# Raw attention rows staged in the weights' rooms, branch weights loaded three ahead, and the place of the last token block's norm

## The chip, the cores and the metric

The kernel runs on one core of a Trainium2 chip. The metric is the device time of one execution in microseconds (us). Three runs of the kernel before took 1567.14, 1567.76 and 1568.34 us, so the median is 1567.76. TensorE is called PE here, VectorE DVE, ScalarE ACT, GpSimd POOL, and SyncE, which issues most transfers, SP.

## The reference

One layer of an encoder on a sequence of 1024 tokens with 1024 channels, in float32. What the change touches is in the merge of the two branches and in the norm ahead of the MLP:

```
h = rmsnorm(x, g_mix)                       # z = h @ w_in -> pooling channels, q, k, v
y_pool = pool_mixer(u_pool, ...)            # 512 channels
y_attn = diff_attention(q, k, v, ...)       # 8 heads x 128 channels, each head's output RMS-normed, * g_sub * 0.8
gates  = sigmoid(h @ w_gate + b_gate)
merged = gates[:, :D] * (y_pool @ w_branch_pool) + gates[:, D:] * (y_attn @ w_branch_attn)
x  = x + merged @ w_out
h2 = rmsnorm(x, g_ffn)                      # x * rsqrt(mean(x*x) + 1e-6) * g_ffn
x  = x + square(relu(h2 @ w_up)) @ w_down
```

## The kernel before

Every float32 operand of a product is split into a high part (a cast on ACT) and a low part (the difference, on DVE or POOL; `split`, L115), and every product is three matmuls: high by high, high by low, low by high (`mm3`, L120, whose three lines L123 to L125 carry nearly all rows of PE).

**Stages.** First the attention runs head by head (8 heads, 8 token blocks of 128 each), with its stages overlapped over the blocks. While it ends, PE also computes the pooling channels and the 16 column tiles of the gates (`gate_cols`), whose results go to DRAM. Then come, in this order: `branch_pool` for the eight output tiles d of the pooling branch (rows `bp`); the attention branch for the eight tiles d (rows `ba`), each with a contraction over the eight heads' tiles `yT[0]` to `yT[7]`, in two halves of 512 tokens; the output projection (rows `op`); the norm ahead of the MLP; the MLP's up projection in 16 column pairs and its down projection. Both MLP projections use Strassen's scheme with seven products (numbered 1 to 7) on blocks of the normed input: 11, 21 and the combinations T1, T2, T3, 22 and T4.

**From the attention to `yT`.** A head's unnormed output goes to DRAM as rows of `y_dram`, and its norm's factors, one per token, as a row of `r_dram` (`stage_norm`, L600; the factors' store is L614). In the loop at L798 each tile is read back: `load_split` (L189) loads raw y (512 KB) into a `raw` tile, loads the head's row of factors broadcast over all partitions (`rb`, L198), scales raw y by them and by `gs` on DVE (L199), and splits it into two tiles `yT`.

**Rooms.** A tile pool has a fixed number of rooms for each tag, and an instruction that writes a new tile waits until a room of the tag is free. `raw` has 2 rooms and serves all raw weights of these stages (`rbp`, `rba`, `ro`), the raw pooling outputs (`rypT`) and raw y (`ryT`). Split weights lie in 8 rooms "W" and 4 rooms "fw" of 4 KB a partition; `wt` (L129) gives the first 64 tiles (the attention's) W rooms, and then by turns 8 tiles W and 4 tiles fw. The gates' weights also use the four fw rooms, with raw rooms of their own (`fr`, two, L142). The factors `rb` use a U room of the attention's (11 of these, which `yT` 0 to 4 use too), the single room `fu`, or two half rooms `fr` and `fo` by `tmp`; `yT` 5 to 7 go to rooms of a pool that is opened when the attention has ended.

**Weights of the attention branch.** `load_cols` loads one tile of `w_branch_attn`; tiles 0, 1 and 2 are loaded in the loop at L798 (L801 to L803), and the loop at L811 loads tile d + 2 for each d, so tile 2 is loaded and split twice.

**The norm ahead of the MLP.** `norm_token` (L903) takes a token block: two squares with sums on ACT, the sum and mean on DVE (L912), EPS added on DVE and the power -1/2 on POOL (`rsq`, L246), a scaling on ACT (L914), the product with the gain row `gfb` on DVE (L917), and eight transposes on PE (L920). `second_half` calls it for blocks 4 to 7 and makes T1 and T2 of a block from the transposed halves and from what `first_half` put into DRAM; `combine` (L989) then makes T1's split, T3, 22 and T4 of all four blocks, on DVE with casts on ACT. The loop at L1111 traces the beginnings of the first four pairs and a call of `combine` behind each.

**The order of the work.** The order on each engine's queue is set when the program is built. A planner runs the program by times of its own and gives each engine, among the instructions that are ready in its time, the one that stands earliest in the program; `tc.cur_priority` moves a piece of program to an earlier place. On the chip each queue then goes in that fixed order, SP's included, and an instruction that has to wait holds all behind it. The last pair of the up projection has its place noted as `last_pair` (L1127), and the first three operand sets of the down projection (`early`, L1255) are given this place.

## Time and profile before

| What | Value |
|---|---|
| median of three runs | 1567.76 us (1567.14 to 1568.34) |
| span of the profiled execution | 1565.6 us |
| the profiled execution's time beside the span | not given by the page; the span is the figure that it has |
| mean granted TensorE clock | 0.996 |
| PE busy | 1536.9 us, 98% of the span |
| DVE, ACT, POOL busy | 1016.4, 817.6 and 357.3 us |
| DMA | 206.94 MB, mean 132 GB/s |

The span runs from the first to the last instruction of one execution, and times in rows are us from its start. A row of a timeline gives start, duration, engine, line, operation, result and operands with buffer numbers left out, shape and count, and in brackets how long the engine had idled and what released it. A row of the list of waits gives total us, times and longest. `SPq` and `ACTq` are issues of transfers; their duration is that of the issue, not of the transfer. PE's matmuls are pipelined: their starts, not their durations, give the pace.

### The profile page before, as it was taken

What the parts mean: (1) busy time and instruction counts of PE and PEld (TensorE: products, weight loads), DVE (VectorE), ACT (ScalarE), POOL (GpSimd) and SP (SyncE); (2) the same over time, 40 slices, a digit from 0 to 9 for tenths busy, and PEclk for the clock granted to TensorE, in tenths of its full rate; (3) what the DMA queues carried; (4) which work ended last, traced back from release to release, by engine and by line L of the source; (5) the groups of instructions that cost most, each with busy time, mean ns of one, the idle gap of its engine ahead of it and who ended that gap; (6) DMA issues with size and microseconds to landing.
All of it is one profiled execution on the core that took longest, in us unless ns stands there. A gap on an engine that the chain in (4) does not pass through costs nothing.

```text
span 1565.6 us, 22082 instructions
## 1 busy us (share of the span) xinstructions
PE 1536.9 (98%) x7649; PEld 1322.5 (84%) x7649; DVE 1016.4 (65%) x2277; ACT 817.6 (52%) x1810; POOL 357.3 (23%) x449
## 2 busy tenths in 40 slices
PE   7999999999999999999799999999999999999999
PEld 6899999999999989888688887888888788888887
DVE  6777677777878797743542358776666568546572
ACT  6656556656565655544542546565555634333331
POOL 5433333343434252222454400000000000000000
PEclk9999999999999999999899999999999999999999
DMA  7111212121112121256645633555342699537650
GB/s 227 50 52 48 64 46 62 34 64 52 60 44 67 35 89 40 69 158 207 205 143 177 193 115 117 182 166 185 132 141 108 247 316 381 197 121 252 218 195 27
DMA packets 168010, 206.94 MB, mean 132 GB/s; under 512 B 10118, under 2 KB 104027, under 8 KB 167899
## 3 DMA queue, kind: packets, MB, share of 16 engines
q1 hardware_dynamic: 150490, 178.23, 35.3%
q10 hardware_dynamic: 17408, 27.30, 4.7%
q8 instruction: 60, 0.98, 0.3%
q14 instruction: 52, 0.42, 0.1%
HBM read 150.94 MB, written 54.56 MB: 131 GB/s over the span
## 4 chain that ended last, share of the span: by engine, by line
PE 49%; DVE 1%; ACT 1%; DMA 1%; issue 1%; POOLq 0%; DVEq 0%
PE Da L124 4%; PE Da L123 4%; PE Da L125 4%; PE Db L124 3%; PE Db L123 3%; PE Db L125 3%; PE X L123 3%; PE X L124 3%; PE X L125 3%; PE ba L124 2%; PE op L123 2%; PE op L125 2%; PE op L124 2%; PE ba L125 2%; PE ba L123 2%; PE Z L123 2%
## 5 line engine op out<-in xcount | busy, mean ns | idle before, releaser
L123 PE MATMUL z<-wqkv,hT 128*128 128x384 f32 x512 | 174.5, 341 | 0.5 <-DVE qn L441 0.3
L125 PE MATMUL z<-wqkv,hT 128*128 128x384 f32 x512 | 174.3, 341 | 0.5 <-DVE hT L118 0.4
L124 PE MATMUL z<-wqkv,hT 128*128 128x384 f32 x512 | 173.6, 339 | 0.0
L510 ACT ACTIVATE s<-s,nm 128x256 f32<-128x256 f32 (+7 forms) x128 | 99.6, 778 | 48.9 <-DVE nm L502 44.0
L249 POOL TENSOR_TENSOR ms<-ms,mhalf 128x4 f32<-128x4 f32 x64 | 67.4, 1053 | 157.8 <-DVE ms L248 139.3
L125 PE MATMUL g<-hT,fwgate 128*128 128x512 f32 x256 | 101.0, 394 | 0.0
L124 PE MATMUL g<-hT,fwgate 128*128 128x512 f32 x256 | 100.9, 394 | 0.0
L123 PE MATMUL g<-hT,fwgate 128*128 128x512 f32 x256 | 100.9, 395 | 0.0
L123 PEld LDWEIGHTS z<-wqkv,hT 128*128 128x128 f32 x512 | 96.8, 189 | 4.2 <-DVE qn L441 1.0
L125 PEld LDWEIGHTS z<-wqkv,hT 128*128 128x128 f32 x512 | 96.6, 189 | 3.1 <-DVE hT L118 1.3
L124 PEld LDWEIGHTS z<-wqkv,hT 128*128 128x128 f32 x512 | 96.7, 189 | 2.9
L502 DVE CUSTOM_DVE_ANT_0 s<-sc,dist 128x512 f32<-128x512 f32 (+3 forms) x128 | 74.7, 586 | 22.1 <-PE sc L500 20.7
L118 DVE TENSOR_TENSOR AS<-s,AS 128x512 fp32r<-128x512 f32 x64 | 43.9, 689 | 36.7 <-ACT AS L117 36.5
L118 POOL TENSOR_TENSOR wqkv<-rqkv,wqkv 128x384 fp32r<-128x384 f32 x60 | 63.1, 1071 | 19.6 <-ACT wqkv L117 19.3
L499 PE MATMUL sc<-K,Q 128*128 128x512 f32 (+2 forms) x192 | 67.2, 355 | 0.1
L500 PE MATMUL sc<-K,Q 128*128 128x512 f32 (+2 forms) x192 | 66.6, 354 | 0.0
L473 ACT CAST Q<-tk 64x128 fp32r<-64x128 f32 x128 | 33.2, 259 | 58.6 <-DVE Q L472 56.8
L447 POOL TENSOR_TENSOR qn<-qn,ggh 128x128 f32<-128x128 f32 x64 | 32.3, 505 | 137.7 <-DVE qn L441 119.5
L470 ACT CAST Q<-tk 64x128 fp32r<-64x128 f32 x128 | 33.0, 258 | 50.1 <-DVE K L469 48.7
L123 PE MATMUL ba<-yT,wba 128*128 128x512 f32 x128 | 51.7, 404 | 7.6 <-ACT yT L117 7.6
L118 POOL TENSOR_TENSOR fwgate<-frgate,fwgate 128x512 fp32r<-128x512 f32 x32 | 45.0, 1408 | 53.7 <-ACT fwgate L117 53.5
L125 PEld LDWEIGHTS g<-hT,fwgate 128*128 128x128 f32 x256 | 48.1, 188 | 8.6
(429 smaller groups left out, 4659.6 us busy)
## 6 DMA issues: line engine op xcount, KB each, us to landing
wd<-in_w_down_dram SPq DMA_DIRECT2D x56, 512.0 KB, 5.6
wu<-in_w_up_dram SPq DMA_DIRECT2D x32, 512.0 KB, 5.0
udS<-us SPq DMA_DIRECT2D x64, 256.0 KB, 2.3
ur<-udS SPq DMA_DIRECT2D x32, 512.0 KB, 3.4
rqkv<-in_w_in_dram SPq DMA_DIRECT2D x64, 192.0 KB, 2.8
ud<-u ACTq DMA_DIRECT2D x48, 256.0 KB, 3.9
ur<-ud SPq DMA_DIRECT2D x24, 512.0 KB, 3.9
frgate<-in_w_gate_dram SPq DMA_DIRECT2D x32, 256.0 KB, 2.7
```

Source lines behind the costliest of these rows:

```text
L118: (lo_eng or nc.vector).tensor_tensor(lo, src, f(hi), op=ALU.subtract)
L123: nc.tensor.matmul(ps, lhs_hi, rhs_hi, start=first, stop=False, **kw)
L124: nc.tensor.matmul(ps, lhs_hi, rhs_lo, start=False, stop=False, **kw)
L125: nc.tensor.matmul(ps, lhs_lo, rhs_hi, start=False, stop=last, **kw)
L249: nc.gpsimd.tensor_tensor(dst, dst, mhalf[:, :n], op=ALU.pow)
L447: nc.gpsimd.tensor_tensor(qn[:, 2:4, :], qn[:, 2:4, :], ggh.unsqueeze(1).broadcast_to([P, 2, HD]), op=ALU.mult)
L470: nc.scalar.copy(q_hi, q)
L473: nc.scalar.copy(Q[other, m, 1, :], q)
L499: nc.tensor.matmul(dst, Q[:, i, 0, :], rhs, start=True, stop=False)
L500: nc.tensor.matmul(dst, Q[:, i, 1, :], rhs, start=False, stop=True)
L502: nc.vector.tensor_tensor_reduce(out=s[i][:, c : c + w], in0=sc[:, 0:w], in1=dist[:, o0 + c : o0 + c + w], scale=2.0 ** -(h + 1), scalar=B ...
L510: nc.scalar.activation(s[i][:, 0:n], s[i][:, 0:n], AF.Exp, bias=last, scale=-1.0, accum_out=Z[:, i, t : t + 1])
```

## The change

- Raw y gets W rooms instead of `raw` (`y_scaled`). Tiles 0 to 3 are loaded and scaled at once behind the first pooling weights in program order, and each tile d + 4 behind the split of tile d. The factors of tiles 0 to 3 and 5 use `fu`, those of 4 a U room, those of 6 and 7 the half rooms.
- The turns of W and fw rooms behind the attention are written out (`ROOMS`, one letter for two tiles): two pooling pairs in W, two in fw, then three attention tiles in W, two in fw and three in W.
- The loop over the attention branch loads tile d + 3 instead of d + 2, so that tile 2 is loaded once.
- `norm_token` computes (sum + D * EPS) to the power -1/2 with one DVE step; the missing factor, the root of D, is multiplied into `gfb` once.
- The instructions of `combine` for T3, 22 and T4 are put behind the last norm's scaling on ACT and its gain product on DVE in these queues (`tc.issue_after`: an order on the same engine, no wait for an end).
- `up_pair` has one more yield behind the copies of products 6 and 5 (U2 and z5). For the last pair the loop steps to this point before `last_pair` is noted.

```diff
+ROOMS = "WWFFWWWFFWWW"
+N_AHEAD_Y = 4
@@ def wt
-        if wcount[0] > N_QKVW and (wcount[0] - N_QKVW - 1) % (N_W + N_FW) >= N_W:
+        if wcount[0] > N_QKVW and ROOMS[(wcount[0] - N_QKVW - 1) // 2] == "F":
             return fw_tile(shape, name)
@@ def load_split
-    def load_split(src, r0, name, tile_fn, scale=None):
-
-        rw = raw([P, S], f"r{name}")
-        nc.sync.dma_start(rw, src[r0 : r0 + P, :])
-        if scale is not None:
-            rbs, row = scale
-            n = S // len(rbs)
-            for i, rb in enumerate(rbs):
-                js = slice(i * n, (i + 1) * n)
-                nc.sync.dma_start(rb, row[js].partition_broadcast(P))
-                nc.vector.scalar_tensor_tensor(rw[:, js], rw[:, js], gs, rb, op0=ALU.mult, op1=ALU.mult)
+    def split_halves(rw, name, tile_fn):
+
         ts = []
         for th in range(2):
             t = tile_fn([P, 2, 512], F32R, f"{name}_{th}", th)
             split(t[:, 0, :], t[:, 1, :], rw[:, th * 512 : (th + 1) * 512])
             ts.append(t)
         return ts
+
+    def load_split(src, r0, name, tile_fn):
+
+        rw = raw([P, S], f"r{name}")
+        nc.sync.dma_start(rw, src[r0 : r0 + P, :])
+        return split_halves(rw, name, tile_fn)
+
+    def y_scaled(d, rbs):
+
+        rw = wpool.tile([P, S], F32, tag="W", name=f"ry{d}", bufs=N_W)
+        nc.sync.dma_start(rw, y_dram[d * P : (d + 1) * P, :])
+        n = S // len(rbs)
+        for i, rb in enumerate(rbs):
+            js = slice(i * n, (i + 1) * n)
+            nc.sync.dma_start(rb, r_dram[d][js].partition_broadcast(P))
+            nc.vector.scalar_tensor_tensor(rw[:, js], rw[:, js], gs, rb, op0=ALU.mult, op1=ALU.mult)
+        return rw
@@
+    def row_factors(d):
+        if d < N_AHEAD_Y or d == 5:
+            return [fu_tile(f"rb{d}")]
+        if d == 4:
+            return [ut([P, S], F32, f"rb{d}")]
+        return [tmp(f"rb{d}_{i}") for i in range(2)]
+
     ws_bp = {0: load_cols2(w_branch_pool, 0, "bp0")}
+    ys = {d: y_scaled(d, row_factors(d)) for d in range(N_AHEAD_Y)}
     ypT = [load_split(p_dram, g * P, f"ypT{g}", ypt_tile) for g in range(4)]
@@
         branch_pool(d, ws_bp[d - d % 2][d % 2], bank)
-        if d % 4 < 2:
-            rb = [fu_tile(f"rb{d}") if d % 2 else ut([P, S], F32, f"rb{d}")]
-        else:
-            rb = [tmp(f"rb{d}_{i}") for i in range(2)]
-        yT.append(load_split(y_dram, d * P, f"yT{d}", yt_tile(d), (rb, r_dram[d])))
+        yT.append(split_halves(ys.pop(d), f"yT{d}", yt_tile(d)))
+        if d + N_AHEAD_Y < NK:
+            ys[d + N_AHEAD_Y] = y_scaled(d + N_AHEAD_Y, row_factors(d + N_AHEAD_Y))
     mT = {}
     for d in range(NK):
-        if d + 2 < NK:
-            ws_ba[d + 2] = load_cols(w_branch_attn, (d + 2) * P, f"ba{d + 2}")
+        if d + 3 < NK:
+            ws_ba[d + 3] = load_cols(w_branch_attn, (d + 3) * P, f"ba{d + 3}")
@@
     nc.sync.dma_start(gfb, g_ffn[0].partition_broadcast(P))
+    nc.vector.tensor_scalar(gfb, gfb, float(D) ** 0.5, None, op0=ALU.mult)
@@ def norm_token
-        nc.vector.tensor_scalar(rs, ss[:, 0:1], ss[:, 1:2], 1.0 / D, op0=ALU.add, op1=ALU.mult)
-        rsq(rs, rs, 1, 1.0)
-        nc.scalar.activation(yn, yn, AF.Copy, scale=rs)
+        nc.vector.tensor_scalar(rs, ss[:, 0:1], ss[:, 1:2], D * EPS, op0=ALU.add, op1=ALU.add)
+        nc.gpsimd.tensor_tensor(rs, rs, mhalf[:, 0:1], op=ALU.pow)
+        last["act"] = nc.scalar.activation(yn, yn, AF.Copy, scale=rs).ins
         for j, b in enumerate(ps):
             js = slice(j * 512, (j + 1) * 512)
-            nc.vector.tensor_tensor(yn[:, js], yn[:, js], gfb[:, js], op=ALU.mult)
+            last["dve"] = nc.vector.tensor_tensor(yn[:, js], yn[:, js], gfb[:, js], op=ALU.mult).ins
@@ def up_pair
         nc.scalar.copy(z5, Z)
+        yield
         sub(dve, S3, A["11"], A["21"])
@@
-        combine(q)
+        with ExitStack() as behind:
+            if q != "T1":
+                for e in last.values():
+                    behind.enter_context(tc.issue_after(e))
+            combine(q)
@@
         if p == NP - 1:
+            next(pairs[p])
             last_pair = tc.cur_priority
```

More of the change, by code (lines that the diff above doesn't have):

```diff
@@ L901, in b_split @@
         split(hi[:, :, c0 : c0 + P], lo[:, :, c0 : c0 + P], src, eng)
+    last = {}
     def norm_token(t, bank_fn):
```

## The prediction

> **What bounds the kernel now.** I read the page's busy shares first, then the list of what TensorE (PE) waited for.
>
> ```profile
> span 1565.6 us, 22082 instructions
> PE 1536.9 (98%) x7649; PEld 1322.5 (84%) x7649; DVE 1016.4 (65%) x2277; ACT 817.6 (52%) x1810; POOL 357.3 (23%) x449
> ```
>
> ```profile
> PE ba L123 <- ACT yT L117: 7.6, 1, 7.6
> PE Z L123 <- ACT BT1h L117: 2.8, 1, 2.8
> PE X L123 <- ACT U L1071: 1.6, 1, 1.6
> ```
>
> PE is busy 98% of the span, so a gain can only be idle or slowed PE time. These waits (total us, times, longest), with one of 1.4 us at the same `ba` product that its timeline shows below, are all above 1 us besides the start of the kernel, which the change doesn't touch. They stand at three places, and the diff has an edit for each: the branch product `ba` waits for `yT`, product 5 (`Z`) waits for the last token's `BT1`, the last pair's product 7 (`X`) waits for the copy U2. I take the places one by one, each from PE's timeline (start, duration, engine and line, idle before and its releaser).
>
> **Place 1, the y tiles.** The first `ba` product runs, stops before its eighth k, and starts again slowly:
>
> ```profile
> 745.11 0.40 PE L123 MATMUL ba<-yT,wba 128*128 128x512 f32 x1
> ...
> 749.30 0.40 PE L123 MATMUL ba<-yT,wba 128*128 128x512 f32 x1
> ...
> 757.94 0.80 PE L123 MATMUL ba<-yT,wba 128*128 128x512 f32 x1 [7.58 <-ACT yT L117]
> 760.10 0.80 PE L124 MATMUL ba<-yT,wba 128*128 128x512 f32 x1 [1.37 <-DVE yT L118]
> ...
> 765.27 0.39 PE L124 MATMUL ba<-yT,wba 128*128 128x512 f32 x1
> ```
>
> The row at 749.30 is the 18th start after 745.11: 4.19 / 18 = 0.233 us each. The row at 765.27 is the 34th, which at that pace would start at 745.11 + 34 x 0.233 = 753.03. So this place costs 765.27 - 753.03 = **12.2 us**: 7.58 + 1.37 of waiting and some 3.3 of slow matmuls. The windows show the slow clock, and none after the 2.8 us wait of place 2 (columns: length, then busy PE, PEld, DVE, ACT, POOL with counts, granted clock, DMA share, GB/s):
>
> ```profile
> 750.00:760.00 10.00, 1.15 (x3) 0.29 (x1) 5.58 (x8) 6.49 (x11) 2.94 (x2) 0.74 0.64 201
> 950.00:960.00 10.00, 8.44 (x39) 6.11 (x37) 8.29 (x15) 3.84 (x6) 3.87 (x1) 1.00 0.10 28
> 960.00:970.00 10.00, 8.79 (x38) 7.12 (x39) 7.22 (x12) 8.52 (x17) 0.00 (x0) 1.00 0.38 110
> ```
>
> The late tile is the eighth. Its raw y shares two `raw` rooms with the branch weights, so its load is issued after PE already needs it:
>
> ```profile
> 668.55 0.34 SPq L198 DMA_DIRECT2D rb<-r_dram  x1
> 669.42 0.37 SPq L671 DMA_DIRECT2D frgate<-in_w_gate_dram  x1
> ...
> 750.25 0.32 SPq L192 DMA_DIRECT2D ryT<-y_dram  x1
> ```
>
> The change takes raw y out of `raw`. When can the eighth be ready now? Its data is complete when head 7's factors are stored, and a load, one scale and a split follow:
>
> ```profile
> 708.87 0.29 ACTq L614 DMA_DIRECT2D r_dram<-rT  x1
> ```
>
> ```profile
> ryT<-y_dram SPq DMA_DIRECT2D x8, 512.0 KB, 4.9
> rb<-r_dram SPq DMA_DIRECT2D x4, 512.0 KB, 3.9
> ```
>
> ```profile
> 698.77 1.28 DVE L199 SCALAR_TENSOR_TENSOR ryT<-ryT,gs,rb 128x1024 f32<-128x1024 f32 x1 [3.52 <-DMA ryT<-y_dram]
> ```
>
> The store's landing isn't shown; 4.9 us, the time of the far larger y load, is my upper bound. 708.87 + 0.29 + 4.9 + 3.9 + 1.28 and as much again for the split is 720.5, some 30 us before PE asks for it near 750. Rooms: weights of head 7 leave eight W rooms, which hold bp0 (2), y0 to y3 and bp2 (2); y4 to y7 follow into the rooms of y0 to y3 as these are split. Even four loads strictly one behind the other, 4 x 4.9 = 19.6 from that store, with 2.6 of scale and split behind them, end some 19 us ahead of the need. That W rooms could be taken from a head's weights too early I exclude: the U room for y0's factors, a row written in head 0, was only granted at 668.55, so rooms are handed out in program order. I take the whole 12.2; the bounds are 0 (nothing arrives sooner) and 12.2.
>
> What is late next there: the weights `ba`, which now have `raw` to themselves and start earlier. Dropping the second load of tile 2 takes away one 512 KB transfer, two casts and two GpSimd (POOL) subtractions that no PE wait names: 0, and at most 0 to 1 if POOL became late. The same four scales and eight splits now run while PE does the gates, before 700. PE had no wait there; if every scale delayed an attention step that PE has in its queue, it would be 4 x 1.28 = 5.1. I take 0, since the gate products fill in, and keep 5.1 for the range.
>
> **Place 2, the last token's norm.**
>
> ```profile
> 939.43 0.69 DVE L845 TENSOR_TENSOR y<-op,y 128x512 f32<-128x512 f32 x1 [3.21 <-PE op L125]
> 942.24 0.59 ACT L910 ACTIVATE nsq<-y 128x512 f32<-128x512 f32 x1
> 943.64 1.29 DVE L118 TENSOR_TENSOR BT3l<-y,BT3h 128x512 fp32r<-128x512 f32 x2
> 948.46 0.21 DVE L912 TENSOR_SCALAR nrs<-nss 128x1 f32<-128x1 f32 x1
> 950.99 0.14 DVE L248 TENSOR_SCALAR nrs<-nrs 128x1 f32<-128x1 f32 x1
> 955.18 1.16 ACT L914 ACTIVATE y<-y,nrs 128x1024 f32<-128x1024 f32 x1 [4.06 <-POOL nrs L249]
> 956.37 1.29 DVE L917 TENSOR_TENSOR y<-y,gfb 128x512 f32<-128x512 f32 x2 [1.63 <-ACT y L914]
> 957.21 1.23 PE L920 MATMUL hb<-identf,y 128*128 128x128 f32 x8
> ```
>
> ```profile
> L249 POOL TENSOR_TENSOR nrs<-nrs,mhalf x8: 545/550/3872, 877.2 to 951.3; 128x1 f32<-128x1 f32 x8
> ```
>
> The second fence is the power on POOL, min/median/max in ns with its last start. The token is complete at 940.12, and its second square starts 2.1 us later, its sum 5.6 us after that, the second small VectorE (DVE) step 2.5 us later still: queues full of combinations and operand splits. The edit drops that second step (its 0.14 and the 2.5 of queue in front of it) and puts the combinations T3, 22 and T4 behind the norm on ACT and DVE. Operand splits and T1 stay ahead. In DVE's queue between 940.0 and 948.4 stand 14 operations; four are combinations (the two at 943.64 and two of `B22`), ten stay, and at 0.60 apart are 6.0 us: the sum comes by 946.2 at the latest, the end of a 3.87 us power by 950.1, that of scaling (1.16), the two products with the gain (1.29) and the eight transposes (1.23) by 953.8; a subtraction, a cast and a split of some 0.69 each make `BT1` by 955.9. PE runs out of work at 957.21 + 1.23 = 958.44. So the 2.8 us go. Against it stands the deferred work: 20 combination operations of 0.60 are 12 us of DVE that now start near 952 instead of 943. DVE idled 20 - 8.29 - 7.22 = 4.5 us between 950 and 970, which is about what can be caught up, and half of the 9 us shift remains to be met by order. I charge 0.8 us for product 4 (T4) coming late and take **2.0**, bounds 2.8 and, if PE then waits for the other half, 2.8 - 4.5 = -1.7.
>
> The last power took 3.87 us, seven times its peers' 0.55, and ended at 955.15; DVE's queue was full until 956.37 - 1.63 = 954.74, as the row of the gain product shows. The Trainium skill, SBUF — State Buffer, section "SBUF: two separate sides", says that GpSimd and VectorE share one pair of ports, held exclusively for a whole instruction when VectorE reads two SBUF inputs. By that rule every DVE queue that is full when the power starts holds it again, here too, and the 3.87 in my sum stays; without it 0.55 would do and the chain would end 3.3 us earlier. Both lie ahead of 958.4, so the sum is the same, but by the rule another 2.6 us of full queue on top would bring the wait back.
>
> Multiplying the gain row by 32 once costs at most the 1.28 of a two-input operation of that size; it lies in the output projection, in which PE waits for nothing: 0, at most 1.3.
>
> **Place 3, the last pair.**
>
> ```profile
> 1244.08 1.04 ACT L117 CAST u_3h<-ur 128x1024 fp32r<-128x1024 f32 x1
> 1245.02 1.04 ACT L117 CAST w_0h<-wd 128x1024 fp32r<-128x1024 f32 x1
> ...
> 1247.86 0.57 ACT L1071 COPY U<-X 128x512 f32<-128x512 f32 x1
> ```
>
> ```profile
> 1248.48 0.50 PE L123 MATMUL X<-BT3h,AS 128*128 128x512 f32 x1 [1.59 <-ACT U L1071]
> ```
>
> Three weight casts of the down projection (w_0 to w_2) stand ahead of the copy that frees `X`. With the new yield those operands rank behind U2 and z5. If the copy goes in front of w_0 it ends at 1245.6, before PE's need at 1248.48 - 1.59 = 1246.9: the whole 1.6. `u_3`, which ranks lower still, went first because it was ready, so one or two casts can stay ahead; with two, 0.8 is left. I take **1.4**, bounds 0 and 1.6. The down projection's first operands move back by two copies, some 1.1 us, which PE's remaining products cover.
>
> **Sum.** 12.2 + 2.0 + 1.4 = 15.6. The span 1565.6 becomes 1550.0. The page gives no time beside the span; the three runs shown have a median of 1567.76, 2.2 more than the profiled span, which I leave unchanged: **1552.2 us**.
>
> **Rivals.** *The y wait only shrinks* (0.11): the new order of SyncE's queue (SP) leaves y7 5 us late instead of 9. For it: SP waits in order, and factors 0 to 3 and 5 pass through one `fu` room. Against it: 30 us of margin. Then 4 us of wait and up to 3.3 of slow clock stay of 12.2: 5 gained, 1567.8 - 5 - 3.4 = 1559.4. The Trainium skill, TensorE: Matmul & The Clock Gate, Part 1, puts the idle time that halves the clock at about 3.4 us, between the 2.8 and 7.6 seen here; by it a rest below that would cost no clock, 3.3 less.
>
> *The combinations become the bound* (0.10): place 2 gives -1.7, and the pair behind it, whose operands DVE makes as well, is late by 2 more, my estimate; 1567.8 - 12.2 - 1.4 + 3.7 = 1557.9. For it: the deferred 12 us; against it the 4.5 idle.
>
> *The change doesn't do what it says* (0.06): the planner, which orders by its own clock, still issues y4 to y7 late; only places 2 and 3 gain, 1564.4, or nothing, 1567.8.
>
> *A hold on SP* (0.08), the side of slower. With factors 0 to 3 in one room, each factor load waits on SP for the scale before it: 3.9 + 1.28 and, as my estimate, 1.8 of gaps, 7 us a step. If three steps stand ahead of the gate load that was issued at 669.42, it comes 21 us late.
>
> ```profile
> 676.83 1.29 POOL L118 TENSOR_TENSOR fwgate<-frgate,fwgate 128x512 fp32r<-128x512 f32 x1 [1.41 <-ACT fwgate L117]
> 682.17 0.69 ACT L745 ACTIVATE go<-g,cols 128x512 f32<-128x512 f32 x1 [1.66 <-PE g L125]
> ```
>
> Those weights were done at 678.1; PE ended the product before at 682.1 and needs their second half 12 matmuls of 0.233 later, at 684.9: 6.8 us of slack. PE then waits 14.2 and pays 3.3 of clock: 1552.2 + 17.5 = 1569.7, with a fourth step 1576.7. It decides from a hold of 19.1 us (6.8 + 15.6 - 3.3). Against it: factor 0 can be loaded long before the W rooms come free, so that the steps can be over before 669.
>
> **How the numbers follow.** My forecast has 0.65, and its own range is 1550.8 to 1555.5 (all three waits whole: 1567.8 - 16.6 = 1551.2, with the runs' half spread; nothing from place 3 and 0 from place 2: 1555.5). To leave out no more than 0.2 with the unknown delays among the gates (5.1 more is 1557.3) the range reaches over the first two rivals to 1561: 1550.5 to 1561. A measurement of this kernel can tell about 0.2%, 3.1 us. Faster by more: 0.65 + 0.11 + 0.10 and half of the third, 0.89; within it the other half and a hold of three steps, 0.06; slower a hold of four or the like elsewhere, 0.05.
>
> **What would show it.** Right: no `ba` wait on `yT` and a clock of 1.00 throughout; raw y loads before 725; PE's wait for `BT1` and for U2 gone from the list. Wrong: a PE wait on `g` or `bp` near 680 to 735 (the SP hold), on `BT4` or `BT3` behind 965 (the combinations), or y7 loaded behind 740. A new wait of over 3 us anywhere would make the forecast wrong, above all in the gates, whose order is planned anew.

## The result, and the profile after

The changed kernel takes a median of 1556.93 us (1556.57 to 1557.44, five runs) against 1567.76 before (1566.17 to 1568.87, five runs): a ratio of 0.9933, 95% interval 0.9921 to 0.9945. It is 10.8 us faster. That lies above the forecast of 1552.2 and its own range (to 1555.5), and within the full range (to 1561.0). The profiled execution took 1556.93 us and has a span of 1555.1, 10.5 less than before.

In the kernel after, lines are shifted: `mm3` is L125 to L127, `split` L119 and L120, the norm L929 to L939, the copy U2 L1090. PE is now busy 99% of the span. This is the list of what it waited for (total us, times, longest):

```profile
PE X L125 <- ACT U L1090: 1.5, 1, 1.5
PE Z L125 <- ACT BT1h L119: 1.4, 1, 1.4
...
PE Y L125 <- DVE u L861: 0.8, 1, 0.8
PE W L125 <- ACT A L119: 0.7, 1, 0.7
```

The two waits of `ba` are gone, and no wait on `g` or `bp` took their place. The wait of X for U2 is where it was. The wait of Z for BT1 is halved, and Y and W wait now, which did not before: 1.40 + 0.82 + 0.75 = 2.97 us at place 2 against 2.76.

Where the 10.5 us lie shows in PE's groups by tile, which give the first and last start of each kind of product (min/median/max in ns ahead of them). Before:

```profile
L123 PE MATMUL z<-wqkv,hT x512: 331/334/689, 10.5 to 626.6; 128*128 128x384 f32 x171
L123 PE MATMUL g<-hT,fwgate x256: 387/392/481, 29.1 to 700.8; 128*128 128x512 f32 x128
L123 PE MATMUL ba<-yT,wba x128: 390/393/796, 745.1 to 845.9; 128*128 128x512 f32 x128
L123 PE MATMUL op<-wo,mT x128: 389/389/477, 846.6 to 938.5; 128*128 128x512 f32 x128
L123 PE MATMUL Da<-w_0h,u_0h x32: 392/392/392, 1254.1 to 1522.6; 128*128 128x512 f32 x32
```

And after:

```profile
L125 PE MATMUL z<-wqkv,hT x512: 331/334/688, 10.9 to 626.7; 128*128 128x384 f32 x171
L125 PE MATMUL g<-hT,fwgate x256: 387/392/497, 29.9 to 701.7; 128*128 128x512 f32 x128
L125 PE MATMUL ba<-yT,wba x128: 392/394/399, 746.0 to 834.9; 128*128 128x512 f32 x128
L125 PE MATMUL op<-wo,mT x128: 389/389/488, 835.6 to 927.5; 128*128 128x512 f32 x128
L125 PE MATMUL Da<-w_0h,u_0h x32: 392/392/392, 1243.5 to 1512.0; 128*128 128x512 f32 x32
```

| Stretch, from these rows | before | after | change |
|---|---|---|---|
| up to the last `z` | 626.6 | 626.7 | +0.1 |
| last `z` to last `g`: the gates | 74.2 | 75.0 | +0.8 |
| first `ba` to first `op` (place 1) | 101.5 | 89.6 | -11.9 |
| last `op` to first `Da` (places 2 and 3) | 315.6 | 316.0 | +0.4 |

The rest, from the first `Da` to the end, is 311.5 and 311.6. So place 1 gave what was forecast, places 2 and 3 gave nothing, and the gates took 0.8 us more.

**The gates.** The 0.8 us arise at one place. Counted from the last `z`, PE's 10th start comes as early as before, the 20th 0.76 us later, and the 390th 0.80 later. Between the 10th and the 20th stands a product (`po`) on the low part of an attention tile, `oqs`, which DVE makes. Before, then after (DVE and PE):

```profile
627.36 0.78 DVE L118 TENSOR_TENSOR oqs<-oq,oqs 128x256 fp32r<-128x256 f32 x1
628.99 0.28 PE L591 MATMUL po<-oqs,ones 128*128 128x256 f32 x1
...
629.56 0.40 PE L123 MATMUL g<-hT,fwgate 128*128 128x512 f32 x1
```

```profile
626.23 1.28 DVE L214 SCALAR_TENSOR_TENSOR ry<-ry,gs,rb 128x1024 f32<-128x1024 f32 x1 [0.50 <-DMA ry<-y_dram]
...
628.67 0.41 DVE L120 TENSOR_TENSOR oqs<-oq,oqs 128x256 fp32r<-128x256 f32 x1
629.14 0.38 PE L601 MATMUL po<-oqs,ones 128*128 128x256 f32 x1
...
630.30 0.50 PE L125 MATMUL g<-hT,fwgate 128*128 128x512 f32 x1
```

The first scale of raw y now stands ahead of that split in DVE's queue. The split ends at 629.08 instead of 628.14, and PE's product starts behind it.

**Place 1** after, in the timeline (the issues of the raw y loads on SP, L209; the store of head 7's factors on ACT, L624; the loads of the last factors on SP, L213) and in the groups of tile `yT`; the third fence is the window that had the clock at 0.74 before:

```profile
622.95 3.75 SPq L209 DMA_DIRECT2D ry<-y_dram  x4
...
696.85 5.84 SPq L209 DMA_DIRECT2D ry<-y_dram  x2
...
714.66 0.29 ACTq L624 DMA_DIRECT2D r_dram<-rT  x1
...
717.03 0.86 SPq L213 DMA_DIRECT2D rb<-r_dram  x2
```

```profile
L120 DVE TENSOR_TENSOR yT<-ry,yT x16: 676/683/1780, 674.1 to 728.0; 128x512 fp32r<-128x512 f32 x16
```

```profile
750.00:760.00 10.00, 10.00 (x44) 8.06 (x43) 3.91 (x4) 5.36 (x10) 6.03 (x5) 1.00 0.51 153
```

The last load of raw y is issued by 702.7 instead of 750.25, the last half is split at 728.7, and PE computes through the window that had 1.15 us of it before.

**Place 2** after, on all engines (the last token block complete at 929.08, its norm, its T1):

```profile
928.39 0.69 DVE L861 TENSOR_TENSOR y<-op,y 128x512 f32<-128x512 f32 x1 [3.44 <-PE op L127]
...
935.29 2.13 POOL L932 TENSOR_TENSOR nrs<-nrs,mhalf 128x1 f32<-128x1 f32 x1 [15.60 <-DVE nrs L931]
...
938.64 1.29 DVE L936 TENSOR_TENSOR y<-y,gfb 128x512 f32<-128x512 f32 x2 [1.62 <-ACT y L933]
939.85 1.89 DVE L864 TENSOR_TENSOR y<-y 128x512 f32<-128x512 f32 x3
...
941.66 1.89 DVE L120 TENSOR_TENSOR B22l<-y,B22h 128x512 fp32r<-128x512 f32 x3
...
942.59 1.03 PE L939 MATMUL hb<-identf,y 128*128 128x128 f32 x8
...
943.47 0.68 DVE L120 TENSOR_TENSOR A<-wu,A 128x512 fp32r<-128x512 f32 x1
...
944.07 1.89 DVE L120 TENSOR_TENSOR BT3l<-y,BT3h 128x512 fp32r<-128x512 f32 x3
...
945.87 0.68 DVE L864 TENSOR_TENSOR t<-hb,t 128x512 f32<-128x512 f32 x1
...
947.60 0.63 ACT L119 CAST BT1h<-t 128x512 fp32r<-128x512 f32 x1
...
948.29 0.51 PE L125 MATMUL Z<-BT1h,AS 128*128 128x512 f32 x1 [1.40 <-ACT BT1h L119]
...
957.48 0.69 DVE L864 TENSOR_TENSOR y<-y 128x512 f32<-128x512 f32 x1 [1.92 <-DMA y<-nd]
```

The transposes end at 943.62, but the subtraction that makes T1 (`t<-hb,t`) starts at 945.87: from 939.85 to 945.87 DVE works on ten operations, nine of them combinations (`y<-y`, `B22l`, `BT3l`) that were put behind the norm's gain product and so stand ahead of T1. The transposes themselves start 2.66 us after the gain products ended (939.93), and PE is not idle ahead of them: they stand in its queue behind other products.

**Place 3** after, on ACT:

```profile
1234.42 1.04 ACT L119 CAST w_0h<-wd 128x1024 fp32r<-128x1024 f32 x1
...
1236.31 1.04 ACT L119 CAST w_2h<-wd 128x1024 fp32r<-128x1024 f32 x1
1237.26 0.57 ACT L1090 COPY U<-X 128x512 f32<-128x512 f32 x1
```

The order is the one of before, with all three casts ahead of the copy.

### The profile page after: what moved, and what is told of

Read it like the earlier page. It is cut to its first block, busy times and chain, and to the rows that moved or that the text cites. A ratio compares the mean times of both kernels' runs of the same rounds, so it can differ in the third digit from the quotient of the medians.

```text
span 1555.1 us, 22054 instructions
## 1 busy us (share of the span) xinstructions
PE 1535.1 (99%) x7649; PEld 1321.5 (85%) x7649; DVE 1012.4 (65%) x2268; ACT 816.0 (52%) x1808; POOL 350.2 (23%) x447
## 4 chain that ended last, share of the span: by engine, by line
PE 89%; DVE 4%; issue 2%; DMA 2%; ACT 2%; POOL 1%; POOLq 0%; SPq 0%; ACTq 0%; DVEq 0%
PE z L125 5%; PE z L127 5%; PE z L126 5%; PE Da L126 4%; PE Da L125 4%; PE Da L127 4%; PE g L125 3%; PE g L126 3%; PE g L127 3%; PE Db L126 3%; PE Db L125 3%; PE Db L127 3%; PE X L125 2%; PE X L126 2%; PE X L127 2%; PE sc L509 2%
## 5 line engine op out<-in xcount | busy, mean ns | idle before, releaser
L125 PE MATMUL z<-wqkv,hT 128*128 128x384 f32 x512 | 174.9, 342 | 0.5 <-DVE qn L451 0.3
L127 PE MATMUL z<-wqkv,hT 128*128 128x384 f32 x512 | 174.7, 341 | 0.5 <-DVE hT L120 0.4
L125 PE MATMUL g<-hT,fwgate 128*128 128x512 f32 x256 | 101.0, 394 | 0.1
L127 PE MATMUL g<-hT,fwgate 128*128 128x512 f32 x256 | 101.0, 395 | 0.0
L125 PEld LDWEIGHTS z<-wqkv,hT 128*128 128x128 f32 x512 | 97.1, 190 | 4.3 <-DVE qn L451 1.0
L127 PEld LDWEIGHTS z<-wqkv,hT 128*128 128x128 f32 x512 | 96.9, 189 | 3.1 <-DVE hT L120 1.2
L120 POOL TENSOR_TENSOR wqkv<-rqkv,wqkv 128x384 fp32r<-128x384 f32 x60 | 63.7, 1078 | 19.8 <-ACT wqkv L119 19.8
L120 DVE TENSOR_TENSOR AS<-s,AS 128x512 fp32r<-128x512 f32 x64 | 43.9, 688 | 36.1 <-ACT AS L119 35.9
L120 POOL TENSOR_TENSOR fwgate<-frgate,fwgate 128x512 fp32r<-128x512 f32 x32 | 43.9, 1376 | 52.3 <-ACT fwgate L119 52.1
L127 PEld LDWEIGHTS g<-hT,fwgate 128*128 128x128 f32 x256 | 48.1, 188 | 8.7
L125 PEld LDWEIGHTS g<-hT,fwgate 128*128 128x128 f32 x256 | 48.2, 188 | 7.4 <-ACT go L755 0.4
```

Source lines behind the costliest of these rows:

```text
L120: (lo_eng or nc.vector).tensor_tensor(lo, src, f(hi), op=ALU.subtract)
L125: nc.tensor.matmul(ps, lhs_hi, rhs_hi, start=first, stop=False, **kw)
L127: nc.tensor.matmul(ps, lhs_lo, rhs_hi, start=False, stop=last, **kw)
```

## The experiments

Every run is timed in five rounds beside the kernel before on the same chip. In the table, ratios are to that; waits are PE's in the profiled execution, in us; the clock is the lowest granted one in a window of 5 us around place 2.

| Kernel | median us | ratio, 95% interval | waits at place 2 | place 3 | clock |
|---|---|---|---|---|---|
| before | 1567.76 | | Z 2.76 | X 1.59 | 1.00 |
| the change | 1556.93 | 0.9921 to 0.9945 | Z 1.40, Y 0.82, W 0.75 | X 1.50 | 1.00 |
| y tiles only | 1557.49 | 0.9925 to 0.9950 | Z 2.76 | X 1.6 | 0.66 |
| norm only | 1567.12 | 0.9988 to 1.0006 | Z 1.40, Y 0.82 | X 1.6 | 0.66 |
| yield only | 1566.89 | 0.9987 to 1.0005 | Z 2.8 | X 1.6 | 0.66 |
| all combinations behind T1, T2 | 1559.80 | 0.9940 to 0.9965 | X 4.64 | X 1.6 | 0.60 |
| early operands behind U2 | 1558.66 | 0.9936 to 0.9961 | Z 1.40, Y 0.83, W 0.91 | Da 1.52, Db 0.9 | 1.00 |
| only 22, T4 behind T1, T2 | 1556.82 | 0.9922 to 0.9946 | X 1.98, Y 0.71 | X 1.64 | 0.66 |
| no deferral | 1557.86 | 0.9931 to 0.9958 | Z 3.01 | X 1.58 | 1.00 |
| y one ahead | 1557.47 | 0.9925 to 0.9950 | Z 1.4, Y 0.8 | X 1.6 | 0.66 |
| no deferral, root on ACT | 1556.62 | 0.9916 to 0.9943 | Z 2.02 | X 1.6 | 0.66 |
| T4's low parts on POOL | 1558.36 | 0.9935 to 0.9960 | Z 1.40, Y 0.82, W 1.81 | X 1.8 | 1.00 |
| the change, root on ACT | 1556.23 | 0.9917 to 0.9942 | Y 0.83, W 0.78 | X 1.53 | 1.00 |
| the same, two casts behind U2 | 1554.84 | 0.9907 to 0.9935 | Y 0.82, W 0.66 | Da 0.85 | 1.00 |

### The three parts by themselves

The y part alone is the changed kernel without these lines:

```diff
-    nc.vector.tensor_scalar(gfb, gfb, float(D) ** 0.5, None, op0=ALU.mult)
...
-        nc.vector.tensor_scalar(rs, ss[:, 0:1], ss[:, 1:2], D * EPS, op0=ALU.add, op1=ALU.add)
-        nc.gpsimd.tensor_tensor(rs, rs, mhalf[:, 0:1], op=ALU.pow)
+        nc.vector.tensor_scalar(rs, ss[:, 0:1], ss[:, 1:2], 1.0 / D, op0=ALU.add, op1=ALU.mult)
+        rsq(rs, rs, 1, 1.0)
...
-        yield
...
-                    behind.enter_context(tc.issue_after(e))
...
-            next(pairs[p])
```

> The change with the parts on the norm and on the last pair left out: only the y tiles in W rooms, four ahead, and the branch weights three ahead. Reading of the two traces (theory): this part alone carries the whole result; the ba stage takes about 89.6 us instead of 101.5, and the 0.8 us lost in the attention tail and the gates belong to it too, so the time is 1567.8 - 11.9 + 0.9 = 1556.8, that is the time of the whole change within 0.5 us. The prediction's sum (rival): this part alone gives 12.2, so 1555.6, and the whole change would have to be 3.4 us faster than it. A third reading, that the norm and the last pair in fact gained and the y part lost more than the trace tells, would show as a time well above 1557.5.

The norm's part alone is the kernel before with the change's lines on `gfb`, `norm_token` and `behind`:

> The kernel before with the norm's part alone: the gain row multiplied once, one DVE step fewer before the power, combinations T3, 22 and T4 put behind the norm's last scaling on ACT and its last product on DVE. Prediction's step: the 2.8 us wait of product Z for BT1 goes, 0.8 comes back at T4, so 2.0 faster, 1565.8. Theory from the two traces: the combinations go into DVE's queue while the transposes still wait on PE, and stand ahead of the last token's T1 subtraction; the wait moves and splits (about 1.4 at Z for BT1, 0.8 at Y, 0.7 at W), so nothing is gained: between 0.4 slower and 0.4 faster, 1567.4 to 1568.2.

The last pair's part alone is the kernel before with two lines:

```diff
         nc.scalar.copy(z5, Z)
+        yield
...
         if p == NP - 1:
+            next(pairs[p])
```

> The kernel before with the last pair's part alone: one yield more in a pair, one step more of the last pair before the down projection's early operands are given their rank. Prediction's step: the 1.6 us wait of product X for the copy U2 shrinks by 1.4, 1566.4. Theory from the two traces: the rank doesn't decide, since the casts are ready when ACT has nothing else to do; the order on every engine stays, the wait stays at 1.5 to 1.6 us, and the time is that of before within 0.3 us.

The y part carries all of the result that the runs can tell: 1557.49, its stretch of `ba` 89.6 us, and its interval covers the change's 0.9933. The other two parts leave the kernel before where it was, with intervals of about 0.1% on either side of 1. The readings of the two traces held, within what the runs spread. Of the prediction's steps, 2.0 us (a ratio of 0.9987) lies just outside the interval of the norm's part; 1.4 us (0.9991) lies inside that of the last pair's part, so there the time alone decides nothing. The trace does: product X waits 1.6 us for U2 as before.

### Rooms or depth

```diff
-N_AHEAD_Y = 4
+N_AHEAD_Y = 1
```

> The whole change with the y tiles loaded one ahead instead of four: they still have rooms of their own among the weights, apart from raw. Theory (what held the eighth y tile was the sharing of two rooms with the branch weights, not the depth): y7 is loaded once y6 is scaled, some 7 us a step behind the last factors at 709, thus before 735, the ba stage stays at 89.6 to 90.5 us, and the time is that of the change within 1 us. Rival (the depth of four carries the gain): the chain load, scale, split of one tile after the other runs to beyond 746, the wait of ba for yT comes back with 4 us or more and with a lowered clock, 1561 or more.

The group of tile `yT` in this kernel:

```profile
L120 DVE TENSOR_TENSOR yT<-ry,yT x16: 677/684/1785, 672.5 to 736.7; 128x512 fp32r<-128x512 f32 x16
```

The last half is split 8.7 us later than with four ahead and still well before the need at 751; `ba` takes 89.6 us again (747.3 to the first `op` at 836.9). So four ahead isn't needed: with the rest of the y part kept, one ahead is enough. Which of the rooms apart, the turns in `ROOMS` and the weights three ahead does how much of it was not tried apart.

### What ate the norm's gain: order on DVE

First, the combinations are put behind the last token block's splits of T1 and T2 too:

```diff
-        split(hi[:, :, c0 : c0 + P], lo[:, :, c0 : c0 + P], src, eng)
+        a = nc.scalar.copy(hi[:, :, c0 : c0 + P], src).ins
+        v = eng.tensor_tensor(lo[:, :, c0 : c0 + P], src, f(hi[:, :, c0 : c0 + P]), op=ALU.subtract).ins
+        if q in ("T1", "T2") and c0 == 3 * P:
+            last["act" + q], last["dve" + q] = a, v
```

> The whole change, and the deferred combinations T3, 22 and T4 are put behind the last token's splits of T1 and T2 as well, on ACT and on DVE, and not only behind its norm. Theory (combinations that enter the queue while the transposes wait are what ate the norm's gain): the waits of Z for BT1 (1.4), Y (0.8) and W (0.7) shrink to under 1 us in sum, last tile of T1 split by about 946 instead of 949.5; the time is 2 us below the change, about 1555. Rival (the deferred combinations themselves are too much for DVE, whatever their place): BT1 is early, but PE then waits for the operands of T3, 22 or T4, some 1 to 3 us behind 960, and the time is that of the change or up to 1 us above it.

It was slower than the change, 1559.80 us. Its timeline (DVE and PE):

```profile
942.60 1.49 DVE L864 TENSOR_TENSOR t<-hb,t 128x512 f32<-128x512 f32 x2 [2.69 <-PE hb L942]
...
960.57 0.69 DVE L864 TENSOR_TENSOR s<-wu,wu 128x512 f32<-128x512 f32 x1
...
961.97 0.79 PE L125 MATMUL X<-BT3h,AS 128*128 128x512 f32 x1 [4.64 <-ACT AS L119]
```

T1's subtraction started at 942.60 instead of 945.87, and Z and Y waited for nothing. But DVE idled 2.69 us for the transposes, then had everything still to do, and reached the sums of the next pair's weights (`s`) only at 960.57; PE waited 4.64 us for their split, and the clock fell to 0.60 as well. My theory named the right place and missed the price. The rival had the price, though at up to 1 us above the change, not 2.9, and for operands of T3, 22 or T4, where it was the weights' sums that came late.

Then only 22 and T4 go behind T1 and T2, while T3 fills the gap (the lines above kept, and):

```diff
-                for e in last.values():
-                    behind.enter_context(tc.issue_after(e))
+                for k, e in last.items():
+                    if k in ("act", "dve") or q != "T3":
+                        behind.enter_context(tc.issue_after(e))
```

> The whole change, but of the deferred combinations only 22 and T4 are put behind the last token's T1 and T2 splits as well; T3 stays behind the norm alone, so that DVE has it to do while the transposes wait. Reading of the run with all three put behind (DVE is full from 940 to 961, and what is not done in its 2.7 us of idle time comes back as late operands of the next pair): DVE has no idle time, the wait of Z for BT1 goes, the operand of product 7 or 4 comes near 959 instead of 961, and 1.5 to 2 us of wait are left of 3.0: the time is about 1 us below the change, 1555.5 to 1556.3. Rival (only the place before Z matters): all of the 2.2 us at Z and Y is gained, 1554.7. Second rival (any later combination delays the pair behind by as much): the time is that of the change or above.

The wait of Z goes, as expected, but X 1.98 and Y 0.71 are left, 2.69 in all instead of 2.97 and not the 1.5 to 2 of the reading. The time is that of the change, as the second rival had it. Between these two orders and the change PE's wait moves from Z to W or X; its sum doesn't fall by more than 0.3, and DVE has the same work to do before it can make the next pair's operands.

### The power on POOL and the place of the transposes

```diff
         with ExitStack() as behind:
-            if q != "T1":
-                for e in last.values():
-                    behind.enter_context(tc.issue_after(e))
             combine(q)
```

> The whole change without the order that puts the combinations T3, 22 and T4 behind the norm: the norm is shorter by one DVE step and the gain row is multiplied once, nothing else of place 2. Prediction's accounting (the second DVE step cost 0.14 and 2.5 of queue in front of it): the norm ends 2.6 earlier than before, the wait of Z for BT1 shrinks from 2.8 to about 0.2 to 0.5, and the time is 2.3 below the version with the y tiles alone, 1555.2. Theory from the traces (the queue in front of the norm's steps is set by the combinations, and the time freed in one place is taken up in the next): the wait shrinks to between 1.4 and 2.8, 0 to 1.4 gained, 1556.1 to 1557.5.

Neither expectation held: the wait of Z didn't shrink at all, 3.01 us. POOL's power, the next gain product on DVE and the transposes on PE in its timeline:

```profile
938.28 5.14 POOL L932 TENSOR_TENSOR nrs<-nrs,mhalf 128x1 f32<-128x1 f32 x1 [18.01 <-DVE nrs L931]
...
944.65 1.29 DVE L936 TENSOR_TENSOR y<-y,gfb 128x512 f32<-128x512 f32 x2 [1.63 <-ACT y L933]
...
946.64 1.03 PE L939 MATMUL hb<-identf,y 128*128 128x128 f32 x8
```

DVE's queue was full until 944.65 - 1.63 = 943.02, and the power of 128 numbers ended at 943.42, 0.40 later. In the change it ended at 937.42, 0.40 behind a queue that was full until 938.64 - 1.62 = 937.02; before, 0.41 behind. Cutting the DVE step ahead of the power made it start sooner and last longer: counted from the complete token block (929.66 here, 940.12 before), it started 2.5 us sooner and ended 1.3 sooner.

These 1.3 us reach the end of the gain products (16.3 us after the token block instead of 17.5), and no further. The transposes start 17.0 us after it, as before (17.1), without idle time on PE: in this order they stand behind other products, and they are the last work in PE's queue ahead of Z. So a shorter norm couldn't make them start sooner, and the wait of Z is set by what follows them.

To test the hold, the power is replaced by a reciprocal on DVE and a root on ACT, in all eight blocks:

```diff
-        nc.gpsimd.tensor_tensor(rs, rs, mhalf[:, 0:1], op=ALU.pow)
+        nc.vector.reciprocal(rs, rs)
+        nc.scalar.activation(rs, rs, AF.Sqrt)
```

> As the version without the deferral (e10_no_defer), but in the norm of all eight tokens the power on POOL is replaced by a reciprocal on DVE and a square root on ACT, so that no step of the norm runs on POOL. Theory (the power can't finish while DVE's queue is full: 5.14 us with the queue full until 943.02, 2.13 with it full until 937.02, 3.87 with it full until 954.74, each ended 0.40 behind the queue's end, and this hold ate what the shorter norm gained): reciprocal and root take under 1 us together, or some 1.5 us more if ACT has something to load for the root, so scaling starts at 939 to 940.5 instead of 943.46; BT1 is ready 3 us sooner, the wait of Z for BT1 falls from 3.0 to 0 to 0.5; of this 1 to 3 us stay, 1555 to 1557 against the 1557.9 of that version. Rival (the queue in front of the norm's steps alone is the cause, the power was long because it waited for something else of the norm, for example the sum's own write): scaling starts about when it did, the wait stays at 2 to 3 us, and the time is that of e10_no_defer. Second rival (DVE has no time left): the wait of Z goes, but products of the next pair wait for AS or A by as much.

```profile
940.38 0.16 DVE L932 RECIPROCAL nrs<-nrs 128x1 f32<-128x1 f32 x1
...
940.81 1.15 ACT L934 ACTIVATE y<-y,nrs 128x1024 f32<-128x1024 f32 x1
...
944.05 1.29 DVE L937 TENSOR_TENSOR y<-y,gfb 128x512 f32<-128x512 f32 x2
```

Scaling starts at 940.81 instead of 943.46. But the gain product then waits in DVE's queue, which nothing holds up any more, and starts only 0.6 us sooner; the transposes start where they did, at 946.55. The wait of Z falls to 2.02, not to 0.5, since DVE has not idled 1.63 us ahead of the gain product and starts T1's subtraction at 947.19 instead of 948.26. The median falls by 1.2 us against the version with the power (1554.94 to 1557.33 against 1557.03 to 1559.69). So the hold is real, and what it costs is DVE's idle time; behind it stand DVE's order and the place of the transposes. ACT loaded a table for the root once, 1.28 us (ACT_TABLE_LOAD at 867.67), ahead of the first of the eight blocks. Both together, the root on ACT and the deferral:

> The whole change, with the norm's power on POOL replaced by a reciprocal on DVE and a square root on ACT, and the combinations T3, 22 and T4 still put behind the norm. Theory (two things ate the gain of place 2: the hold of the power by a full DVE queue, 2.13 us here, and combinations that stand ahead of the last token's T1 on DVE; taking the hold away lets scaling start up to 2 us sooner and DVE, which idled 1.62 us there, work on): the wait of Z for BT1 falls from 1.4 to 0 to 0.5 and the 0.8 at Y goes; 0.7 to 2 us of wait stay behind 955, since DVE is full; 1554.5 to 1556. Rival (DVE's load is the whole bound there): the waits move behind 955 and the sum stays at 3 us, 1556.5 to 1557.

This kernel is the change with the diff above. DVE's idle time ahead of the gain product falls from 1.62 to 0.26 us, and the wait of Z is gone; Y 0.83 and W 0.78 stay: 1.61 us instead of 2.97. The sum is in the theory's bounds, though the wait at Y, which was to go, is still there; the time is a little outside them. Its median, 1556.23, is only 0.7 below the change, within what its five runs spread (1555.44 to 1557.88).

Can POOL take work off DVE there? The four low parts of T4 on POOL:

```diff
-                b_split(q, c0, b22, dve)
+                b_split(q, c0, b22, pool)
```

> The whole change with the four low parts of the T4 combination made by POOL instead of DVE (POOL has nothing to do there; a POOL subtraction of this size took 1.29 us among the gates). Theory (DVE is full between 940 and 961, and a POOL instruction gets no turn while DVE's queue is full of operations with two inputs from SBUF): each of the four takes several us instead of 1.29 or ends only when DVE idles; they end no sooner than 958, product 4 gets its operand late, and the 2.4 us taken from DVE bring 0 to 1 us at best: 1556.5 to 1559. Rival (DVE's load alone counts, POOL runs beside it): the four take 1.3 to 1.6 us each, the operands of the next pair come 2 us sooner, the waits at W and Y go, 1555.4.

```profile
949.00 4.70 POOL L120 TENSOR_TENSOR BT4l<-y,BT4h 128x512 fp32r<-128x512 f32 x3 [11.41 <-ACT BT4h L119]
...
960.82 0.69 DVE L864 TENSOR_TENSOR s<-wu,wu 128x512 f32<-128x512 f32 x1 [2.05 <-POOL BT4l L120]
```

The time is in the theory's range, but POOL's part went as the rival had it: POOL did get its turn (4.70 / 3 = 1.57 us each instead of 1.29, and 1.29 for the fourth), and DVE's splits beside it, at 949.64 and 952.47, took 1.20 and 1.78 us instead of 0.68. The next pair's sums then waited for the last POOL part, and W for them, 1.81 us.

### The last pair

```diff
-        nc.scalar.copy(U2, X)
+        u2c["act"] = nc.scalar.copy(U2, X).ins
...
-    early = {q: operands("1", q) for q in range(3)}
+    with tc.issue_after(u2c["act"]):
+        early = {q: operands("1", q) for q in range(3)}
```

> The whole change, and the casts of the down projection's early operands are put behind the last pair's copy U2 in ACT's queue by an explicit order instead of a rank. Theory (the casts in front of the copy are the whole of that wait, and the rank can't move them): the 1.5 us wait of product X for U2 goes, 0 to 0.3 is left, the time is 1.2 to 1.5 below the change, 1555.4 to 1555.7 by its 1556.9. Rival (the copy is late for another reason, for example ACT waits for a DMA of a weight tile there, or the early casts are late for the first down product instead): the wait stays above 1 us or comes back as a wait of the first down product, and the time is that of the change.

```profile
1235.16 0.59 ACT L1092 COPY U<-X 128x512 f32<-128x512 f32 x1 [3.97 <-DMA ud<-u]
...
1244.99 0.50 PE L125 MATMUL Da<-w_0h,u_0h 128*128 128x512 f32 x1 [1.52 <-DVE u L861]
```

The copy no longer made PE wait, but ACT stood idle 3.97 us ahead of it with six casts behind it; DVE's six splits followed late (1236.73 to 1243.7), the last pair's sums behind these, and `Da` waited 1.52 and `Db` 0.9 us. That was the rival, and the time rose by 1.7 us besides. With the root on ACT, and only the casts of the second and third weight tile behind the copy:

```diff
-        nc.scalar.copy(U2, X)
+        u2c["act"] = nc.scalar.copy(U2, X).ins
...
-            split(hi, lo, src, dve)
+            with ExitStack() as behind:
+                if n == "w" and j == "1" and q:
+                    behind.enter_context(tc.issue_after(u2c["act"]))
+                split(hi, lo, src, dve)
```

> As e17_root_and_defer, and of the down projection's early operands only the casts of the second and third weight tile are put behind the last pair's copy U2, so that the first tile and the u tiles stay in front. Theory (the version with all operands behind the copy lost its 1.5 us again because DVE then split them just ahead of the last pair's sums, and PE waited for those): two casts of 0.95 fewer in front of the copy take 1.0 to 1.5 us off the wait of X; of this 0.5 to 1.5 stay: that much below e17_root_and_defer. Rival (any operand moved behind the copy delays the last pair's sums or the first down product by as much): a new wait of Da of 0.5 to 1.5 us, and the time of e17_root_and_defer within 0.5.

```profile
1233.30 0.58 ACT L1093 COPY U<-X 128x512 f32<-128x512 f32 x1
...
1242.04 0.50 PE L125 MATMUL Da<-w_0h,u_0h 128*128 128x512 f32 x1 [0.85 <-DVE u L861]
```

The copy follows the first weight cast, X waits no more, and 0.85 us comes back at `Da`, so each side had a part of it; the time, 1.4 us below the version before it, is the theory's. At 1554.84 us (1554.22 to 1555.33) this is the fastest version. All its runs lie below the lowest of that version on the same chip, 1555.44, and below the lowest of the change, 1556.57; the intervals of the ratio overlap.

## Why the prediction was right and where it was not

**The number.** The time lies in the full range because place 1 came as forecast and because the range was drawn over two rivals; the forecast's own sum missed it by 4.7 us. Of the signs that were to show it right, no wait of `ba`, early loads of raw y (by 702.7) and a clock of 1.00 came true; the waits for BT1 and U2 stayed.

**Place 1: right.** 12.2 was forecast, 11.9 measured. The eighth tile ready by 720.5 was too early, it was 728.7, well inside the margin of 30: head 7's factors were stored 5.8 us later than before (714.66 instead of 708.87), and SP issued the loads of the last factors from 717.03 on. The raw loads took 5.6 to 6.9 us, not 4.9, but were long done. The term that was wrong is the one set to 0: the scales and loads among the gates. The gates took 74.2 us in each of the three kernels without the y part and 74.9 to 75.0 in each of the eleven with it, so 0.8 us is its price, inside the 5.1 kept as a bound. The prediction named the mechanism, a scale that delays an attention step which PE has in its queue, and gave it nothing; one of the four scales, the first, did that. The eleven traces agree in this, the version with one tile ahead too, so the depth is not its cause; no run takes that scale out of DVE's way.

**Place 2: the step that failed is "a subtraction, a cast and a split of some 0.69 each make BT1".** Up to the transposes the sum held, by luck: they end 14.5 us after the token is complete (943.62 - 929.08), 13.7 were forecast (953.8 - 940.12). The gain products ended 1.6 us sooner than forecast, 10.85 us after the token instead of 12.45, since the power took 2.13 and not 3.87; and the transposes then stood 2.66 us in PE's queue, for which the sum had nothing. The next three operations were to take 2.1 us more; the high part of BT1 came 4.6 us after the transposes (948.23). Of this the subtraction waited 2.25 us in DVE's queue and the cast 1.05 behind two copies on ACT. I had assumed the combinations to come behind BT1; the edit puts them behind the gain product only, and while the transposes wait on PE, DVE goes on with them. With T1 ahead of them, Z didn't wait in two versions, so this is the cause at Z; the wait came back at X. The charge of 0.8 for a late T4 met its size by chance: product 4 (W) did wait 0.75 us, but for its other operand, A. The idea that 4.5 us of DVE's idle time could be used also failed: some of it is a wait for the transfer `nd`, ahead of the last T4 subtraction, 1.46 us before and 1.92 after.

The prediction also held that the hold of the power brings the wait back only if some 2.6 us of full queue come on top. In the version without the deferral the power was 1.3 us longer than in the sum (5.14 instead of 3.87), and the wait was whole again, because of the transposes' place on PE and not of the power. The Trainium skill, SBUF — State Buffer, section "SBUF: two separate sides", says that GpSimd and VectorE share one port pair, taken for a whole instruction. The traces agree that one holds the other, and here for longer than one instruction: the power got no turn among three, six and eight DVE operations (2.13, 3.87 and 5.14 us, each ended 0.40 to 0.41 behind DVE's full queue). With the power off POOL the wait of Z fell in both pairs of versions that differ in this alone: 3.01 to 2.02, and 1.40 to 0.

**Place 3: the step that failed is "with the new yield those operands rank behind U2 and z5", as far as it was to move the copy.** The rank is a preference among what is ready, and the casts stayed ahead of the copy, at a time for which ACT has nothing else to do (it idled 3.97 us when they were kept back). The yield alone left the order on ACT and the wait of X as they were; an explicit order moved both, and its version with two casts kept 0.7 of the 1.5 us in the waits.

**The rivals.** The nearest was that the combinations become the bound (1557.9), with the right engine and less of a loss: places 2 and 3 together +0.4 instead of +2.3. The SP hold did not come: no wait on `g` or `bp`. The sum's error is 15.6 - 10.5 = 5.1 us: 0.3 at place 1, 0.8 + 0.1 ahead of it, 3.4 + 0.4 at places 2 and 3, and 0.1 at the end.

## What to carry to other kernels

Count how far a deferred piece of work is really deferred: an order behind one instruction lets it in at the next gap of that queue, ahead of everything later in the chain. Where an engine is nearly full over a stretch, as DVE here behind the norm, reordering moves the wait to another product; here only a change that spared DVE idle time made it shorter. Before you shorten a chain, look at the queue in which its next step stands: the transposes started when PE came to them, however early the norm was ready. And a tile that shares its rooms with a stream of others is late by that stream: the rooms apart, with the weights' turns and lead that go with them, were worth far more here than loading it deeper.

## What the runs showed of the hardware

**A small POOL operation can last as long as DVE's queue.** Before, the power on 128 numbers took 0.55 us for each of the seven earlier token blocks, where DVE was idle or had an operand in PSUM, where PE writes its products; it took up to 5.14 us where DVE's queue was full of operations with both operands in SBUF. Larger POOL subtractions, among DVE operations of which some read PSUM, got their turns (1.57 us each) and slowed DVE's (1.20 and 1.78 us).

**A short wait sometimes costs clock, and a wait of the same length in another trace does not.** The window of 5 us right behind the wait of Z, first in the version with the y tiles only (it waited 2.76 us there), then in the one without the deferral (3.01; columns as in the prediction):

```profile
950.00:955.00 5.00, 4.92 (x14) 3.87 (x15) 3.45 (x7) 5.00 (x12) 0.00 (x0) 0.66 0.11 8
```

```profile
950.00:955.00 5.00, 4.32 (x18) 3.49 (x19) 4.62 (x8) 5.00 (x11) 0.00 (x0) 1.00 0.00 0
```

The clock fell to 0.66 behind waits of 2.76 (y only, yield only), 2.02, 1.98 and 1.40 + 0.82 us (norm only, one ahead), and stayed at 1.00 behind 3.01, behind 2.76 (before) and behind 1.40 + 0.82 (the change). The price shows between kernels with the same waits: from the last `op` to the first `Da` 317.1 us with the y tiles only and 317.0 with the yield only, against 315.6 before, some 1.5 us; 0.66 over 5 us is 1.7 us of missing clock. So waits can be compared only with the clock beside them: with the norm only and with y one ahead W didn't wait, but the clock fell, and the stretch took 316.0 and 315.9 us, as in the change (316.0). Executions of one kernel differ too: the five runs of the version without the deferral had mean granted clocks of 0.998 to 1.000. The prediction's "no slow clock after the 2.8 us wait" rested on one execution. The Trainium skill, TensorE: Matmul & The Clock Gate, Part 1, describes a free-running window of about 3.4 us, which agrees with a drop that depends on the execution; that a whole idle window of that length is needed does not agree with 1.98 us.
